# Modulation steps between the router's products, routing weights by f32r passes, and tokens in two f32r parts in the second expert stage

## The chip, the cores and the metric

The kernel runs on one core of a Trainium2 chip. The metric is the device time of one execution in microseconds (us), the median of several runs. A profile of one execution is at hand, with every instruction's start and duration.

## The reference, cut to what matters

A two-layer transformer over 256 latent and 256 context tokens, model width 1024, everything in float32. Layer 0 mixes tokens by window attention, layer 1 by differential attention, and each layer ends in a mixture of 32 experts of which every token uses two. All sub-layers are scaled and shifted by vectors that come out of a "modulation" product.

```
for i in range(2):
    mod  = (silu(c) @ mod_w[i] + mod_b[i]).reshape(6, D)        # shift, scale, gate, shift, scale, gate
    modc = (silu(c_ctx) @ mod_w[i] + mod_b[i]).reshape(6, D)
    h  = rmsnorm(x, g[i, 0]) * (1 + mod[1]) + mod[0]            # hc the same with modc
    y, yc = window_attention(...) if i == 0 else diff_attention(...)
    x = x + mod[2] * y
    h  = rmsnorm(x, g[i, 1]) * (1 + mod[4]) + mod[3]
    # hier_moe: best of 4 groups, two best of its 8 experts, softmax weights w1, w2
    x = x + mod[5] * sum over the token's two experts e of  w_e * (silu(u1) * u2) @ w_down[e],  [u1 u2] = h @ w_up[e]
return rmsnorm(x, final_g)
```

Layer 0 routes 512 tokens (latent and context), layer 1 only the 256 latent ones. Each expert's `w_up` is 1024 x 1024 and its `w_down` 512 x 1024, so one expert is 6.29 MB and one layer's experts are 201 MB.

## The kernel before, in words

**Memory.** SBUF holds an arena of 43 slots of 512 KB (128 partitions x 1024 floats). `Slot()` takes the slot that has been free longest, `free()` puts it at the end. Every weight block is one slot: `plan` is the list of all blocks in the order of use, and `stream.next()` issues the next block's load on SyncE's queue (line 177) into the slot it is given. A load waits until that slot's last reader is done, so how far loads run ahead of use is set by how many slots are free for them.

**Order.** Blocks of code under `tc.manual_schedule(engines=PE)` keep TensorE's instructions in the written order; elsewhere, and on the other engines everywhere, a planner orders them before the run.

**Modulation.** The first two sixths of layer 0 come first, in quarters. Then there are twelve steps in `mod_steps`, four for each third (m = 1, 2: the rest of layer 0; m = 3: shift and scale of layer 1's mixer). One step (`mod_step`, line 370) takes four slots of `mod_w` and makes 8 matmuls in four column strips of the array; a profile counts each float32 matmul as two records, so 16. After a third's last step, `mod_finish` copies the 128x512 sum out of PSUM, turns it by four transposes and adds the bias. Four steps run between the query projections (`QM`), eight inside the first layer's attention (`MODS = range(0, 24, 3)`, that is one in every third of its 24 units; three units are one head pair).

**Router and gather.** `Post` collects a layer's residual stream into 128-token tiles `tok[t]` while the output projection runs. Where a tile is kept in two slots, it is split into two float32r parts (high part by ScalarE, remainder by VectorE; layer 0's four tiles); where it is kept whole (`WHOLE[1] = (0, 1)`, both tiles of layer 1), it is one float32 copy. `moe` then computes logits, finds the experts by a chain of small VectorE operations, and makes ranks (line 1018) from which a 0/1 matrix P is built that picks up to 64 tokens for each of two experts. `gather` multiplies P with the tokens, half of the columns at a time (`half`, line 1152), scales or copies the result (1156 to 1162), turns it back (`spread_tokens`, 1198, 1200), and `gather_weights` (line 1188) multiplies P with the routing weights `WR` as float32 (two or three columns) and copies out one column for each expert (1191, 1193).

**Expert pair.** For each of 16 pairs in each layer: up products (`up`, 1209, 16 slots), `gate`, gather for the next pair, down products (`down`, 1252, 8 slots), weighting (1277, 1278), and `combine` (1291) back to all tokens with `gated_add` (509). At pair 5 a branch asks whether an expert has more than 64 tokens; here it isn't taken.

Of the kernel before, what the change touches and what calls it, by code (L numbers as in the profile page):

```python
# [12 lines left out]
F32 = mybir.dt.float32  # L13
# [12 lines left out]
KT = D // 128  # L26
# [15 lines left out]
WHOLE = ((), (0, 1))  # L42
FILL1 = ((1, 1, 1, 0), (0, 1, 1, 0))
QM = (1, 3, 5, 7)
MODS = range(0, 24, 3)
# [11 lines left out]
def _hybrid_dit(ctx, tc, a, out):  # L57
# [6 lines left out]
               for c, dt in (("f", F32), ("r", F32R))] for i in range(SLOTS)]  # L64
    const = ctx.enter_context(tc.tile_pool(name="const", bufs=1))
# [172 lines left out]
    for c in range(2):  # L238
        for k in range(4):
            plan_cols(wq0, 512 * c, (2 * k,))  # L240
            if 4 * c + k in QM:
                plan_mod(*todo.pop(0))
    while todo:
        plan_mod(*todo.pop(0))
    plan_out(a["win_w_o"][0])
# [58 lines left out]
    ident2 = const.tile([128, 64], F32, name="ident2")  # L304
# [3 lines left out]
    ident_b = const.tile([128, 128], BF, name="ident_b")  # L308
# [10 lines left out]
    for t, op in enumerate((OP.is_gt, OP.is_lt)):  # L319
        m = const.tile([128, 128], BF, name=f"mask_b{t}")  # L320
        ve.tensor_scalar(m, diff_f, 0.0, -BIG, op0=op, op1=OP.mult)
        mask_b.append(m)
# [56 lines left out]
    def mod_finish(l, third, halves, hb, acc):  # L379
        h0, nh = halves[0], len(halves)  # L380
        sb = row("q")
        ve.tensor_copy(sb[hb], acc[hb])
        tp = bank("G")
# [449 lines left out]
    tmp.free()  # L833
    rooms.pop().free()
# [21 lines left out]
    class Post:  # L856
        def __init__(self, l, nt, lb=None):
# [23 lines left out]
            homes[l].slot.free()  # L881
# [29 lines left out]
        def flip(self, h, tags, ks=range(4)):  # L911
            for t in range(self.nt):
# [7 lines left out]
                if t < 2 and len(self.tok[t]) > 1:  # L920
                    hi, lo = (v[:, hs] for v in self.tok[t])
                    se.activation(hi, ps[:, cs], AF.Copy)
                    ve.tensor_tensor(lo, ps[:, cs], hi.bitcast(F32), op=OP.subtract)
                elif self.nr == 1:
                    se.activation(self.slots[t][-1].f()[:, hs], ps[:, cs], AF.Copy, scale=self.ri[:, t:t + 1])
# [55 lines left out]

    def moe(l, nt, post, after, finish):
        T = nt * 128
        with tc.manual_schedule(engines=PE):
            lg = post.logits()
        post.shift(2, ge)
# [38 lines left out]
        WR = const.tile([128, nt, NE // 2, 3], F32, name=f"WR{l}", tag="WR")  # L1025
        W = WR[:, :, :, 0:2]
        cmi = const.tile([128, 1], I32, name=f"cmi{l}", tag="cmi")

        def weights():
# [22 lines left out]
            if not unit:  # L1052
                ve.tensor_copy(WR[:, :, :, 2], post.ri.unsqueeze(2).to_broadcast([128, nt, NE // 2]))
        h_slots, tok, unit = post.slots, post.tok, post.nr == 1

        np_ = NE // 2
        prev = st = None
        early_ks = range(0, KT // 2) if T == 512 else ()
        late_ks = range(len(early_ks), KT)
        for p in range(np_):  # L1060
# [17 lines left out]
            if p == IF_AT:  # L1078
# [6 lines left out]
                with tc.If(most > CAP):  # L1085
                    overflow(l, nt, key, W, None if unit else post.ri, tok, [hs_[k // 2].f(2, 512)[:, k % 2] for k in range(KT)])
# [39 lines left out]
    def gather(l, nt, p, key, WR, tok, unit, early=None, between=None, ri=None):  # L1126
# [10 lines left out]
        if ri is not None:  # L1137
            st["P"] = P
            if not unit:
                wps = bank("G")  # L1140
                for t in range(nt):
                    pe.matmul(wps[:, 0:1], P[:, t, :].bitcast(F32), ri[:, t:t + 1], start=(t == 0), stop=(t == nt - 1))
                ve.tensor_copy(st["w"][:, 1:2], wps[:, 0:1])
# [39 lines left out]

    def gather_weights(P, WR, p, st, n):
        wps = bank("G")
        nt = P.shape[1]
        for t in range(nt):
# [110 lines left out]
    def overflow(l, nt, key, W, ri, tok, hT):  # L1298
        T = nt * 128
        for t in range(nt):  # L1300
            for h in range(2):
# [13 lines left out]
                for k in range(4):  # L1315
# [3 lines left out]
        ve.scalar_tensor_tensor(Wov.rearrange("p t (a b) -> p t a b", b=2),  # L1319
                                key.rearrange("p t (a b) -> p t a b", b=2), float(CAP), W,  # L1320
# [484 lines left out]
```

## Time and profile before

| | |
|---|---|
| median of 3 runs | 1551.51 us (1550.75 to 1552.95) |
| the profiled execution's own time | 1550.44 us |
| its span, first to last instruction | 1548.8 us |
| mean granted TensorE clock | 0.981 of full speed |
| TensorE matmuls busy (PE) | 1458.1 us, 94% |
| VectorE (DVE), ScalarE (ACT), GpSimd (POOL) busy | 655.5, 384.6, 184.2 us |
| read from HBM | 483.16 MB, 313 GB/s over the span |

PE counts matmuls, PEld the loading of the stationary operand beside them. Busy times are unions; the ends of matmuls are modelled, so a row of matmuls is best read from the start of one group to the start of the next. "Idle before" names what an engine waited for.

### The profile page before, as it was taken

The page shows a single profiled execution, that of the slowest core. Times are in us where ns is not written, and L with a number is a line of the kernel's source. Part 1 is how long each engine was busy: PE and PEld are TensorE (multiplying, and loading weights), DVE is VectorE, ACT ScalarE, POOL GpSimd, SP SyncE. Part 2 cuts the span into 40 slices and gives each one's busy share as a digit, 9 for nine tenths or more (in the row PEclk, how much of TensorE's full clock was granted, in tenths as well). Part 3 has the DMA queues.
Part 4 walks back from the last instruction along what each step waited for, and adds up shares of the span by engine and source line. Part 5 has one row for each costly group of instructions (what it writes and reads, how often), then busy time and mean ns, then how long its engine had stood idle before and what let it go on. Part 6 is the DMA issues. An engine that isn't in the chain of part 4 may idle for free. (4 is left out here: it accounts for less than half of the span.)

```text
span 1548.8 us, 20271 instructions
## 1 busy us (share of the span) xinstructions
PE 1458.1 (94%) x7463; PEld 800.3 (52%) x7463; DVE 655.5 (42%) x1585; ACT 384.6 (25%) x823; POOL 184.2 (12%) x147
## 2 busy tenths in 40 slices
PE   6998999799999999999999899798999899999997
PEld 4765567445444454444545678684434333433444
DVE  3338862424333443333448726863323222322323
ACT  4426653211010011101115235652101010110112
POOL 2314551000000000000006463100000000000000
PEclk9999999899999999999998999999999999999999
DMA  9767225799989999999996532488999999999991
GB/s 330 243 214 273 82 86 187 278 366 401 395 343 393 401 398 398 391 397 403 382 297 229 182 124 71 161 284 304 387 409 409 409 408 409 409 409 409 409 394 68
DMA packets 169695, 485.67 MB, mean 314 GB/s; under 512 B 20825, under 2 KB 41586, under 8 KB 169586
## 3 DMA queue, kind: packets, MB, share of 16 engines
q1 hardware_dynamic: 169088, 483.66, 82.2%
q8 instruction: 63, 1.03, 0.3%
q10 hardware_dynamic: 498, 0.60, 0.1%
q14 instruction: 46, 0.38, 0.1%
HBM read 483.16 MB, written 1.05 MB: 313 GB/s over the span
## 5 line engine op out<-in xcount | busy, mean ns | idle before, releaser
L1209 PE MATMUL ps<-slotf,row 128*64 128x512 f32 x2048 | 449.2, 593 | 2.1 <-DVE row L1200 2.1
L1209 PEld LDWEIGHTS ps<-slotf,row 128*64 128x64 f32 x2048 | 145.2, 137 | 289.7 <-issue 274.4
L1252 PE MATMUL ps<-slotf,row 128*64 128x512 f32 x960 | 212.6, 595 | 0.0
L546 PE MATMUL ps<-slotr,slotr 128*128 128x512 f32 x768 | 193.4, 405 | 13.4 <-DVE slotf L1414 6.7
L509 DVE SCALAR_TENSOR_TENSOR slotf<-ps,mod,slotf 128x256 f32<-128x256 f32 x408 | 167.3, 477 | 62.3 <-PE ps L1291 29.7
L546 PEld LDWEIGHTS ps<-slotr,slotr 128*128 128x128 f32 x768 | 145.1, 194 | 50.4 <-DVE slotf L1414 7.1
L1252 PEld LDWEIGHTS ps<-slotf,row 128*64 128x64 f32 x960 | 66.3, 137 | 124.9 <-issue 118.9
L1216 ACT ACTIVATE row<-ps 128x512 f32<-128x512 f32 x30 | 17.9, 597 | 425.9 <-PE ps L1209 386.6
L1217 DVE SCALAR_TENSOR_TENSOR row<-row,ps 128x512 f32<-128x512 f32 x30 | 20.6, 687 | 234.4 <-ACT row L1216 234.3
L1278 DVE SCALAR_TENSOR_TENSOR row<-ps,ty,row 128x512 fp32r<-128x512 f32 x60 | 45.0, 750 | 176.5 <-ACT row L1277 173.3
L1277 ACT ACTIVATE row<-ps,ty 128x512 fp32r<-128x512 f32 x60 | 41.3, 688 | 263.0 <-PE ps L1252 262.7
L1291 PE MATMUL ps<-row,row 128*128 128x512 f32 (+1 forms) x512 | 104.4, 348 | 1.1 <-DVE slotf L509 1.0
L1291 PEld LDWEIGHTS ps<-row,row 128*128 128x128 f32 x512 | 77.3, 189 | 36.5 <-ACT row L1216 21.1
L521 POOL TENSOR_TENSOR slotr<-slotf,slotr 128x1024 fp32r<-128x1024 f32 x32 | 78.9, 2479 | 86.9 <-ACT slotr L517 72.1
L1200 DVE TENSOR_TENSOR row<-ps,mod 128x512 f32<-128x512 f32 x64 | 42.7, 686 | 101.7 <-PE ps L1198 100.9
L481 POOL TENSOR_TENSOR row<-row,row 128x512 f32<-128x512 f32 (+1 forms) x13 | 15.0, 1156 | 575.6 <-PE ps L1291 519.4
L1152 PE MATMUL ps<-slotf,row 128*128 128x512 f32 x128 | 65.0, 632 | 7.0 <-PEq L1085 4.7
L1152 PE MATMUL ps<-slotr,row 128*128 128x512 f32 x256 | 70.4, 419 | 0.0
L517 ACT ACTIVATE slotr<-slotf 128x1024 fp32r<-128x1024 f32 x44 | 45.9, 1055 | 63.1 <-DMA slotf<-in_diff_w_qkv 38.0
L1152 PEld LDWEIGHTS ps<-slotr,row 128*128 128x128 f32 x256 | 47.9, 198 | 10.0 <-issue 0.8
L1377 PE MATMUL ps<-slotr,slotr 128*128 128x512 f32 x192 | 47.6, 399 | 0.0
L1198 PE MATMUL ps<-ident,row 128*128 128x128 f32 x256 | 37.8, 280 | 7.5 <-DVE row L1156 6.7
(314 smaller groups left out, 1526.8 us busy)
## 6 DMA issues: line engine op xcount, KB each, us to landing
slotf<-in_moe_w_up SPq DMA_DIRECT2D x512, 512.0 KB, 9.5
slotf<-in_moe_w_down SPq DMA_DIRECT2D x256, 512.0 KB, 10.2
slotf<-in_mod_w SPq DMA_DIRECT2D x96, 512.0 KB, 6.3
slotf<-in_diff_w_qkv SPq DMA_DIRECT2D x24, 512.0 KB, 3.9
slotf<-in_win_w_qkv SPq DMA_DIRECT2D x12, 512.0 KB, 5.2
slotf<-in_win_w_o SPq DMA_DIRECT2D x8, 512.0 KB, 4.0
slotf<-in_diff_w_o SPq DMA_DIRECT2D x8, 512.0 KB, 4.1
slotf<-in_x SPq DMA_DIRECT2D x2, 512.0 KB, 4.1
```

The costliest lines, as they stand in the source:

```text
L509: ve.scalar_tensor_tensor(xT[k][:, sl], ps[:, sl], g[:, k, r:r + 1], xT[k][:, sl], op0=OP.mult, op1=OP.add)
L517: se.activation(hv, v, AF.Copy)
L521: (eng or (ge if split_i[0] % 3 == 0 else ve)).tensor_tensor(lv, v, hv.bitcast(F32), op=OP.subtract)
L546: pe.matmul(ps[t], h[:, x, ts], w[y][:, kk, :], start=(k + kk == 0 and n == 0), stop=(k + kk == KT - 1 and n == 2))
L1152: pe.matmul(g, P[:, t, :] if len(tok[t]) > 1 else P[:, t, :].bitcast(F32), v[:, hs], start=(t == 0 and i == 0), stop=(t == nt - 1 and i == ...
L1200: ve.tensor_tensor(o.rearrange("p (k c) -> p k c", k=4), ps.rearrange("p (k c) -> p k c", k=4), mods[l][:, 3, 4 * h:4 * h + 4, 0:1].to_bro ...
L1209: pe.matmul(u[h][64 * s:64 * s + 64, :], st["xt"][k // 4][:, c0:c0 + 64], w[s][1][:, h * 512:(h + 1) * 512], start=(k == 0), stop=(k == KT ...
L1252: pe.matmul(y[h][64 * s:64 * s + 64, :], acT[:, c0:c0 + 64], w[s][1][:, h * 512:(h + 1) * 512], start=(k == 0), stop=(k == 3))
L1277: se.activation(yh, y[h], AF.Copy, scale=wsl)
L1278: ve.scalar_tensor_tensor(yl, y[h], wsl, yh.bitcast(F32), op0=OP.mult, op1=OP.subtract)
L1291: pe.matmul(out, part[:, c * 128:(c + 1) * 128], st["PT"][:, :T], start=(i == 0), stop=(i == 1))
L1377: pe.matmul(ps, w[x][:, k % 4, ms], oT0[k][1][:, y, :], start=(k == 0 and i == 0), stop=(k == KT - 1 and i == 2))
```

## The change

- Four of the eight modulation steps leave the first layer's attention (`MODS` takes every sixth unit). Their 16 weight blocks are planned after the output projection's weights instead of before. In `moe` of layer 0 three of the four steps run right after the logits, in a bank of group A (`mods_meanwhile`), the fourth after the rank products (`last_mods`); its sum is copied by ScalarE, and `mod_turned` runs after the first gather. The slot `homes[0]`, which holds its bias, is freed after that instead of in `Post`.
- `WR` becomes float32r with a high and a low part; `gather_weights` is one float32r matmul for a tile, over 4 (layer 1) or 6 (layer 0) columns, in place of a float32 one. The two parts are added while they are copied out, by ScalarE with its accumulator (`add_parts`), in place of VectorE's copies. The factor 1/rms of layer 0's first pair goes the same way (`rr`).
- `WHOLE[1]` is empty: layer 1's two tiles are kept in two float32r parts in four slots instead of two, split from PSUM by ScalarE (with its scale) and VectorE (one `scalar_tensor_tensor`), and `half` takes two float32r matmuls for a tile instead of one float32 matmul.
- `ident2`, `ident_b` and the two masks move from storage of their own into one slot, `masks`, which is held from the start to the end of the first layer's attention.

```diff
-WHOLE = ((), (0, 1))
+WHOLE = ((), ())
-MODS = range(0, 24, 3)
+MODS = range(0, 24, 6)
...
+    while len(todo) > KT // 2:
+        plan_mod(*todo.pop(0))
+    plan_out(a["win_w_o"][0])
     while todo:
         plan_mod(*todo.pop(0))
-    plan_out(a["win_w_o"][0])
     plan_experts(0)
...
+    masks = Slot()
+    ident2 = masks.f()[:, 0:64]
...
     def mod_finish(l, third, halves, hb, acc):
-        h0, nh = halves[0], len(halves)
         sb = row("q")
         ve.tensor_copy(sb[hb], acc[hb])
+        mod_turned(l, third, halves, hb, sb)
...
-            homes[l].slot.free()
+            if not mod_steps:
+                homes[l].slot.free()
...
+                    if self.nr == 1:
+                        ri = self.ri[:, t:t + 1]
+                        se.activation(hi, ps[:, cs], AF.Copy, scale=ri)
+                        ve.scalar_tensor_tensor(lo, ps[:, cs], ri, hi.bitcast(F32), op0=OP.mult, op1=OP.subtract)
...
+    def mods_meanwhile():
+        while len(mod_steps) > 1:
+            mod_step("A")
+
+    def last_mods():
+        l, third, halves, hb, acc = mod_step("A").args
+
+        def moved():
+            sb = row("q")
+            se.activation(sb[hb], acc[hb], AF.Copy)
+            return partial(mod_turned, l, third, halves, hb, sb)
+
+        return moved
...
             lg = post.logits()
+            mods_meanwhile()
...
             pe.matmul(cps[:, 0:NE], ones_b, Mb[:, t, :], start=(t == 0), stop=(t == nt - 1))
-        WR = const.tile([128, nt, NE // 2, 3], F32, name=f"WR{l}", tag="WR")
-        W = WR[:, :, :, 0:2]
+        moved = last_mods() if mod_steps else None
+        cols = 2 if unit else 3
+        WR = const.tile([128, nt, NE // 2, 2, cols], F32R, name=f"WR{l}", tag="WR")
+        if not unit:
+            rr = const.tile([128, nt, 2], F32R, name=f"rr{l}")
+            ve.tensor_copy(rr[:, :, 0], post.ri)
+            ve.tensor_tensor(rr[:, :, 1], post.ri, rr[:, :, 0].bitcast(F32), op=OP.subtract)
...
+            hi, lo = WR[:, :, :, 0, :], WR[:, :, :, 1, :]
+            se.activation(hi, wide_w, AF.Copy)
+            ve.tensor_tensor(lo, wide_w, hi.bitcast(F32), op=OP.subtract)
...
+        turn_mods = moved() if moved else lambda: None
...
-                    st = gather(l, nt, 0, key, WR, tok, unit, weights, ri=post.ri)
+                    st = gather(l, nt, 0, key, WR, tok, unit, weights, ri=() if unit else rr)
+                    turn_mods()
+                    if moved:
+                        homes[l].slot.free()
...
+    def add_parts(dst, src):
+        n = src.shape[0]
+        se.activation(tiny("ap", [128, 2], bufs=2)[:n], src, AF.Copy, accum_out=dst)
+
     def gather_weights(P, WR, p, st, n):
...
-            pe.matmul(wps[:, 0:n], P[:, t, :].bitcast(F32), WR[:, t, p, 0:n], start=(t == 0), stop=(t == nt - 1))
+            pe.matmul(wps[:, 0:2 * c], P[:, t, :], WR[:, t, p], start=(t == 0), stop=(t == nt - 1))
+        v = wps[:, 0:2 * c].rearrange("p (b c) -> p c b", b=2)
         for s in range(2):
             pb = slice(64 * s, 64 * s + 64)
-            ve.tensor_copy(st["w"][pb, 0:1], wps[pb, s:s + 1])
+            add_parts(st["w"][pb, 0:1], v[pb, s])
         if n == 3:
-            ve.tensor_copy(st["w"][:, 1:2], wps[:, 2:3])
+            add_parts(st["w"][:, 1:2], v[:, 2])
```

## Rows read from the trace of the kernel before

**Rows 1.** The page: its first part (busy time, share of the span and instructions of each engine) and, of its second, the GB/s that the DMA engines moved in 40 equal slices of the span (38.7 us each).

```profile
PE 1458.1 (94%) x7463; PEld 800.3 (52%) x7463; DVE 655.5 (42%) x1585; ACT 384.6 (25%) x823; POOL 184.2 (12%) x147
...
GB/s 330 243 214 273 82 86 187 278 366 401 395 343 393 401 398 398 391 397 403 382 297 229 182 124 71 161 284 304 387 409 409 409 408 409 409 409 409 409 394 68
```

**Rows 2.** Busy time by stretch in the second layer's expert stage: the stretch in us from the span's start, its length, for each engine the busy us and (in brackets) instructions, then the granted TensorE clock as a share of full speed, the DMA engines' busy share, and GB/s.

```profile
1080.00:1120.00 40.00, 38.93 (x188) 17.17 (x188) 12.08 (x26) 4.70 (x9) 0.00 (x0) 1.00 0.98 389
1120.00:1480.00 360.00, 348.85 (x1676) 148.74 (x1674) 104.86 (x218) 41.41 (x74) 0.00 (x0) 1.00 1.03 409
...
1500.00:1512.00 12.00, 12.00 (x60) 4.57 (x62) 2.90 (x5) 1.37 (x2) 0.00 (x0) 1.00 1.02 350
1512.00:1516.00 4.00, 4.00 (x20) 1.29 (x18) 0.00 (x0) 0.00 (x0) 0.00 (x0) 1.00 0.67 221
```

**Rows 3.** The chain of waits that ended last, in the second expert stage: start us, length us, what (xcount). One pair of experts of sixteen, and the last pair's up products.

```profile
1259.13 2.10 PE ps L1291 x16
1261.23 1.73 PE ps L1152 x4
...
1263.05 0.61 ACT row L1158
...
1263.70 2.00 PE ps L1152 x4
...
1266.47 1.09 PE ps L1198 x8
...
1274.58 13.73 PE ps L1209 x64
1288.31 2.11 PE ps L1291 x16
...
1508.04 13.73 PE ps L1209 x64
```

**Rows 4.** Busy time by stretch in the first layer's attention; each stretch is one head pair with its three units. Columns as in rows 2; the last line holds sums and means over all four.

```profile
196.52:208.45 11.93, 11.93 (x87) 6.97 (x86) 10.03 (x27) 8.10 (x24) 6.97 (x6) 1.00 0.15 45
sum 47.71, PE 47.71 PEld 27.85 DVE 39.85 ACT 30.24 POOL 26.67; mean PE 11.93 PEld 6.96 DVE 9.96 ACT 7.56 POOL 6.67
```

**Rows 5.** Timeline of TensorE in the same stage, around one modulation step (line 370): start us, us, engine, line, operation, tiles, form, count.

```profile
203.82 1.04 PE L370 MATMUL ps<-slotf,slotf 128*32 128x512 f32 x2
204.79 0.66 PE L785 MATMUL ps<-ident,row 128*128 128x128 f32 x4
205.38 1.92 PE L370 MATMUL ps<-slotf,slotf 128*32 128x512 f32 x14
207.23 0.72 PE L748 MATMUL ps<-slotr,slotr 128*128 128x512 f32 x2
```

**Rows 6.** Timeline of the first layer's router and first gather. In brackets: idle us before it and what ended that.

```profile
281.73 1.19 PE L950 MATMUL ps<-ident,row 36*128 36x36 f32 x8 [0.46 <-ACT row L938]
...
291.02 0.18 PE L1018 MATMUL ps<-Mb,before_b 128*128 128x32 bf16 x1 [8.10 <-DVE Mb L1013]
...
292.65 1.84 PE L1142 MATMUL ps<-ri,row 128*128 128x1 f32 x8 [1.09 <-DVE s L1031]
...
294.35 3.76 PE L1152 MATMUL ps<-slotr,row 128*128 128x512 f32 x8
...
294.60 0.69 DVE L978 TENSOR_TENSOR slotr<-slotf,slotr 128x512 fp32r<-128x512 f32 x1
...
300.38 3.65 PE L1209 MATMUL ps<-slotf,row 128*64 128x512 f32 x16 [0.78 <-DVE row L1200]
```

**Rows 7.** Busy time by stretch across that router, columns as in rows 2.

```profile
284.40:298.05 13.65, 5.94 (x31) 4.98 (x31) 11.62 (x46) 4.05 (x8) 2.52 (x2) 0.50 0.70 272
```

**Rows 8.** Timeline of one gather of the first expert stage.

```profile
318.06 1.05 PE L1188 MATMUL ps<-WR,row 128*128 128x3 f32 x8
...
318.97 2.09 PE L1152 MATMUL ps<-slotr,row 128*128 128x512 f32 x8
...
320.90 0.60 PE L1168 MATMUL ps<-ident,row 128*128 128x128 f32 x4
321.15 0.69 ACT L1162 ACTIVATE row<-ps,ty 128x512 f32<-128x512 f32 x1 [3.21 <-PE ps L1152]
```

**Rows 9.** Busy time by stretch: one pair of the first expert stage, from its down products to the next pair's; columns as in rows 2.

```profile
356.10:387.90 31.80, 31.52 (x155) 15.12 (x154) 12.19 (x28) 3.86 (x6) 0.00 (x0) 1.00 1.01 399
```

**Rows 10.** Groups of instructions by line: busy us, mean ns of one | idle us before them.

```profile
L753 ACT ACTIVATION_READ_ACCUMULATOR row<-ps,ty 128x1 f32 x32 | 6.5, 203 | 0.0
...
L768 ACT ACTIVATE ty<-ty 128x2 f32<-128x2 f32 (+1 forms) x24 | 4.9, 204 | 0.0
```

**Rows 11.** Timeline of the second layer's router and first gather.

```profile
1051.54 2.42 ACT L925 ACTIVATE slotf<-ps,ri 128x512 f32<-128x512 f32 x4 [0.53 <-PE ps L917]
...
1054.76 0.23 DVE L1013 TENSOR_TENSOR Mb<-row,row 128x64 bf16<-128x64 f32 x1
...
1056.20 3.46 PE L1152 MATMUL ps<-slotf,row 128*128 128x512 f32 x4 [0.89 <-DVE s L1031]
...
1061.85 3.65 PE L1209 MATMUL ps<-slotf,row 128*64 128x512 f32 x16 [0.85 <-DVE row L1200]
```

**Rows 12.** Timeline of the loads that SyncE's queue issued (SP) in the first layer: start us, us over which the count was issued, line, tile<-input, count. These are loads of the first expert weights.

```profile
242.49 20.59 SPq L177 DMA_DIRECT2D slotf<-in_moe_w_up  x11
```

**Rows 13.** What the DMA queue (SP) waited for before it could issue the next load, from 0 to 120 us: total us, times, longest us.

```profile
SPq L177 <- PE ps L546: 35.8, 13, 5.7
```

More of the change, by code (lines that the diff above doesn't have):

```diff
@@ L64, in _hybrid_dit @@
                for c, dt in (("f", F32), ("r", F32R))] for i in range(SLOTS)]
+    halves = [nc.alloc_sbuf_tensor_at(f"slotb{i}", [128, 2048], BF, offset=base + 4096 * i).ap() for i in range(SLOTS)]
     const = ctx.enter_context(tc.tile_pool(name="const", bufs=1))
@@ L303, in _hybrid_dit @@
     make_identity(nc, ident)
-    ident2 = const.tile([128, 64], F32, name="ident2")
+    masks = Slot()
+    ident2 = masks.f()[:, 0:64]
+    masks_b = halves[masks.s].rearrange("p (a n) -> p a n", n=128)
     ve.tensor_tensor(ident2, ident[:, 0:64], ident[:, 64:128], op=OP.add)
@@ L307, in _hybrid_dit @@
     ve.memset(ones, 1.0)
-    ident_b = const.tile([128, 128], BF, name="ident_b")
+    ident_b = masks_b[:, 8]
     ve.tensor_copy(ident_b, ident)
@@ L319, in _hybrid_dit @@
     for t, op in enumerate((OP.is_gt, OP.is_lt)):
-        m = const.tile([128, 128], BF, name=f"mask_b{t}")
+        m = masks_b[:, 9 + t]
         ve.tensor_scalar(m, diff_f, 0.0, -BIG, op0=op, op1=OP.mult)
@@ L379, in mod_finish, with mod_turned @@
     def mod_finish(l, third, halves, hb, acc):
-        h0, nh = halves[0], len(halves)
         sb = row("q")
         ve.tensor_copy(sb[hb], acc[hb])
+        mod_turned(l, third, halves, hb, sb)
+    def mod_turned(l, third, halves, hb, sb):
+        h0, nh = halves[0], len(halves)
         tp = bank("G")
@@ L833, in _hybrid_dit @@
     tmp.free()
+    masks.free()
     rooms.pop().free()
@@ L1052, in weights @@
             if not unit:
-                ve.tensor_copy(WR[:, :, :, 2], post.ri.unsqueeze(2).to_broadcast([128, nt, NE // 2]))
-        h_slots, tok, unit = post.slots, post.tok, post.nr == 1
+                ve.tensor_copy(wide_w[:, :, :, 2], post.ri.unsqueeze(2).to_broadcast([128, nt, NE // 2]))
+            hi, lo = WR[:, :, :, 0, :], WR[:, :, :, 1, :]
+            se.activation(hi, wide_w, AF.Copy)
+            ve.tensor_tensor(lo, wide_w, hi.bitcast(F32), op=OP.subtract)
+        h_slots, tok = post.slots, post.tok
         np_ = NE // 2
         prev = st = None
+        turn_mods = moved() if moved else lambda: None
         early_ks = range(0, KT // 2) if T == 512 else ()
@@ L1085, in moe @@
                 with tc.If(most > CAP):
-                    overflow(l, nt, key, W, None if unit else post.ri, tok, [hs_[k // 2].f(2, 512)[:, k % 2] for k in range(KT)])
+                    overflow(l, nt, key, WR, None if unit else post.ri, tok, [hs_[k // 2].f(2, 512)[:, k % 2] for k in range(KT)])
                 for s in hs_:
@@ L1141, in gather @@
                 for t in range(nt):
-                    pe.matmul(wps[:, 0:1], P[:, t, :].bitcast(F32), ri[:, t:t + 1], start=(t == 0), stop=(t == nt - 1))
-                ve.tensor_copy(st["w"][:, 1:2], wps[:, 0:1])
+                    pe.matmul(wps[:, 0:2], P[:, t, :], ri[:, t, :], start=(t == 0), stop=(t == nt - 1))
+                add_parts(st["w"][:, 1:2], wps[:, 0:2])
         elif not unit:
```

16 lines of the change are left out of this document (10 added, 6 removed).

## The prediction, made before the changed kernel was run

> **What bounds the kernel now.** First the page: TensorE's matmuls are busy 94% of the span, so at first sight every matmul taken away is time won; but the GB/s slices rise to a flat 409 in the last quarter, and a flat line is a ceiling [rows 1]. So each stage has to be read by itself, and the last one first.
>
> *Second expert stage.* The stretches show 409 GB/s for 360 us on end at a DMA share of 1.03, with TensorE busy for 349 of them [rows 2]. Both look full. The chain settles which one is: it runs through TensorE and the short copies between its products, never through a load, and one pair takes 29.18 us (from 1259.13 to 1288.31) [rows 3]. A pair's 24 slots are 24 x 0.524 = 12.58 MB, at 409 GB/s 30.8 us. So TensorE uses weights faster than they arrive and lives on the slots loaded ahead. What is left of that lead at the end: after 1500 us the loads move 12 x 350 + 4 x 221 kB = 5.1 MB [rows 2]; the last eight slots (4.2 MB, down weights) are therefore still to come at about 1502.5, and the last up weights have landed then. Their matmuls start at 1508.04 + 7/8 x 13.73 = 1520.05 [rows 3]. The lead is 17.5 us: TensorE can win that much here and then waits for loads.
>
> *First layer's attention.* A head pair takes 11.93 us with TensorE busy throughout; VectorE needs 9.96 us of it, the others less [rows 4]. TensorE is the bound, VectorE next.
>
> *Router of layer 0.* TensorE idles 8.10 us while VectorE finds the experts, and then works at a granted clock of 0.50, that is 1.2 GHz: eight matmuls of line 1152 take 3.76 us [rows 6, 7], against 1.93 from start to next start at the full clock [rows 8].
>
> *First expert stage.* 31.8 us a pair, TensorE busy for 31.52 [rows 9]; loads would need 30.8, so TensorE bounds it, with 1 us to spare.
>
> **The change, part by part.** The sum is made against the profiled execution (1550.44 us, of which 1.64 lie outside the span), 1.07 below the median of the runs.
>
> *Four steps out of the attention.* One step costs TensorE 0.97 us (two records, 203.82 to 204.79) and 1.85 (fourteen, 205.38 to 207.23): 2.82 [rows 5], so 11.3 for four. But a head pair without a step has 9.11 us of matmuls and VectorE 9.96 on average [rows 4]. If VectorE then sets the pace, each saves 1.97. I take that, -7.9; ends -11.3 and -4 (half of it, since scores, softmax and transposes of a unit follow one another and the steps also filled such waits).
>
> *The steps in the router.* Three run in the 8.10 us of idling (3 x 1.85 = 5.6), hidden by VectorE's chain; without that cover they would cost their 5.6. The fourth, 1.85, comes after the rank products, ends near 293.4 and holds up the product behind it (line 1142, start 292.65 before) by 0.7. For the gain: with TensorE at work in the gap I expect the full clock afterwards. Line 1142 then takes under 0.5 instead of 1.84; the gather's remainder for the last tile is ready at 294.60 + 0.69 = 295.3, so its eight products end near 295.8 instead of 298.1 [rows 6]. VectorE's two extra small operations (`rr`) take back 0.3. Term -1.9. If the clock falls all the same, the fourth step (3.7 us at 1.2 GHz) pushes all behind it: +1.6. The turning (four transposes) falls into the wait for VectorE that ends at 300.38 [rows 6]. The 16 mod loads take the places of the first 16 expert loads in SyncE's queue; eleven of those places were issued from 242.49 to 263.08 [rows 12], 20 us ahead of the router, so the steps find their weights. The expert loads behind them come 16 x 1.28 = 20.5 us of transfer later, but the four steps free their slots before the first pair starts, and the first stage's loads need 30.8 us a pair of 31.3: no starving, cost 0.
>
> *Routing weights.* In the first stage line 1188 takes 0.91 us for eight records (318.06 to 318.97) [rows 8]. Four float32r matmuls of 6 columns: no such row; from below 0.114 a record as here, from above 0.131 as line 1291's 256 columns (2.10 us for 16, [rows 3]). I take 0.46, gain 0.45 a pair, 15 pairs: -6.8 (bounds -5.8 and, at half a record's time, -10). The copies move from VectorE (off the path) to ScalarE, each an ACTIVATE and an accumulator read, 0.204 + 0.203 us [rows 10]; three are 1.2 us. Who waits: the scaling (1162) for the third, and the transposes of P (1168) for the bank. Both also wait for the first half's eight products, 1.93 us [rows 8], so 1.2 is hidden; without this cover it would be up to 0.7 a pair.
>
> *Two parts in the second stage.* Each half of a gather is four float32 records, 1.73 us [rows 3]; four float32r matmuls go by 1.93/8 = 0.24 each [rows 8], 0.97. In a pair the way from the first half's start to the turning back (1261.23 to 1266.47, 5.24 us [rows 3]) becomes 0.97, then the six transposes that the copy of 0.61 hid (0.9), 0.97, and copy and issue 0.76: 3.6. TensorE alone saves 1.65 x 15 pairs and 0.9 in the first: 25.6. Loads don't allow it. The lead is 17.5; two slots fewer for loads (four for tokens) put the last load 2 x 1.28 = 2.6 us later; and the loads, no longer held up by slots in the first pairs (389 for 409 GB/s over 40 us [rows 2]), win 2.0 back. Term -17.0 (ends -14 and -19.5).
>
> *Router of layer 1.* No steps here. The first half-gather, 3.46 us at the low clock [rows 11], is halved: -1.7. The remainders are new on VectorE: four of 128x512, 0.69 each by line 978's row [rows 6], ready as ScalarE's four copies end between 1052.1 and 1054.0, in the midst of the chain that ends with Mb at 1054.76 [rows 11]. If the planner puts them in as they become ready, +2.8. I take both: +1.0 (ends -1.7 and +2.8).
>
> *The slot for masks* leaves one less until the attention ends: 0, since TensorE isn't held up by loads there; rival below. The rest costs nothing: the wider copies of `WR` are made while the first up products run.
>
> Sum: -7.9 - 1.9 - 6.8 - 17.0 + 1.0 = -32.6. 1550.44 - 32.6 = 1517.8, on the runs' median 1518.9; I say **1519**.
>
> **Rivals.**
>
> *A: loads give way.* If they ran faster once slots come free sooner, the second stage would give all of TensorE's 25.6 instead of 17.0: 1510. Against it, 409 flat at share 1.03 over 360 us [rows 2]. The Trainium skill (HBM Reference, Specifications) gives about 425 GB/s for a core streaming alone, and 358 as its share. By 425 a layer's 201 MB would come 18 us sooner (an estimate from that page) and this rival would hold; the trace's 409 lies between the two and decides.
>
> *B: the attention gives nothing.* VectorE or the units' own waits take the steps' place, above all near the start where a step covers a wait: 1519 + 7.9 = 1527. For it, VectorE's 9.96 of 11.93 [rows 4]; against it, its share would be 100%.
>
> *C: the steps lengthen the router.* If their loads could start only as the logits are turned (281.73 [rows 6]), 20.5 us of transfer end at 302, the last step starts 10 us later than at 291.5, and the steps are on the path: +10, 1529. Against it, [rows 12].
>
> *D: slower.* The masks' slot is missing in the query projections, where SyncE waited 13 times for slots that line 546 frees, 35.8 us in all, 5.7 at most [rows 13]. If each of eight weight blocks then came 5.7 us later with TensorE waiting, +45.6: 1565. It decides from 32.6/8 = 4.1 us a block, if none of it is cover. Against it, no wait of TensorE for a load there.
>
> **How the numbers follow.** Chances: forecast 0.64, A 0.06, B 0.15, C 0.08, D 0.04, gains that cancel to no change 0.03. Within 0.2% (3.1 us, about what a measurement here can tell from none): 0.03. Slower: D and 0.01 of C's tail, 0.05. Faster: 0.92. The forecast's own ends, put together as independent, are 1513 to 1525; with B and C at 1527 and 1529, and A at 1510, the range is 1509 to 1531.
>
> **What would show it.** Right: head pairs without a step near 10 us; granted clock 1.00 in most of the first router; four records of line 1188's successor in about 0.46 us; pairs of the second stage near 27.6 us until the last one or two, where TensorE waits for `in_moe_w_up`, with 409 GB/s from the stage's start. Wrong: any wait of TensorE for loads before the last third of that stage; pairs that stay at 29 us; pairs of the first stage at 32; a wait for `in_mod_w` in the router; projections held up before 115 us.

## The result

The changed kernel takes 1526.12 us (median; 1522.09 to 1528.14), the kernel before beside it 1551.76: a ratio of 0.9831, 95% interval 0.9809 to 0.9853. On a second chip it was 0.9837 (0.9824 to 0.985). The forecast was 1519 with a range of 1509 to 1531. So the sign and the range held, and of the 32.6 us that the terms add up to, some 26 came.

The page of the changed kernel: its first part and the GB/s of the second, as in [rows 1] (40 slices, here of 38.2 us).

```profile
PE 1431.4 (94%) x7363; PEld 793.2 (52%) x7363; DVE 649.0 (43%) x1512; ACT 410.4 (27%) x986; POOL 184.8 (12%) x147
...
GB/s 326 222 223 139 42 56 193 346 409 409 409 409 408 408 409 409 409 409 408 402 315 228 173 124 83 133 278 265 394 409 409 408 409 409 409 409 409 409 409 199
```

TensorE has 26.7 us less of matmuls, ScalarE 25.8 us more. The flat 409 GB/s now fills both expert stages.

By stages, each taken from the start of a first product to the start of the next stage's (us; the second execution is of the same kernel, `e5_same_again` below):

| stage | before | changed | second execution | change | forecast |
|---|---|---|---|---|---|
| start to the first scores of the attention | 115.53 | 116.20 | 113.08 | +0.7 / -2.5 | 0 |
| attention and out-projection, to the logits' turning | 166.20 | 165.30 | 163.77 | -0.9 / -2.4 | -7.9 |
| router of layer 0 | 18.65 | 17.19 | 17.17 | -1.5 | -1.9 |
| first expert stage, to the start of its last pair | 481.0 | 470.6 | 470.7 | -10.4 | -6.8 |
| from there to layer 1's first up product | 280.5 | 281.5 | 281.5 | +1.1 | +1.0 |
| second expert stage, to the last pair's down products | 463.7 | 452.4 | 452.6 | -11.3 | -17.0 |
| the end | 23.2 | 23.2 | 23.2 | 0 | 0 |

The profiled execution of the changed kernel is the slowest of its runs; in its out-projection the clock was at 0.50 for 3.41 us, which the second execution doesn't show, and that is most of what sets the two apart there.

**Attention.** Busy time by stretch, one head pair each, columns as in [rows 4]; then TensorE's timeline around one modulation step, as in [rows 5] (lines have moved: the step is 375 now, scores 756, transposes 793 and 800, value products 815).

```profile
149.44:160.24 10.80, 10.34 (x72) 6.59 (x71) 9.24 (x29) 7.25 (x23) 6.12 (x6) 1.00 0.00 1
160.24:172.18 11.94, 11.94 (x83) 6.94 (x82) 8.44 (x24) 7.27 (x23) 6.12 (x6) 1.00 0.07 20
...
195.49:207.71 12.22, 9.89 (x69) 6.50 (x68) 12.22 (x37) 8.34 (x24) 6.13 (x6) 1.00 0.11 39
```

```profile
155.77 1.04 PE L375 MATMUL ps<-slotf,slotf 128*32 128x512 f32 x2
156.75 0.66 PE L793 MATMUL ps<-ident,row 128*128 128x128 f32 x4
...
159.65 0.66 PE L800 MATMUL ps<-ident,slotf 128*128 128x128 f32 x4 [0.34 <-POOL slotf L797]
...
166.57 1.05 PE L375 MATMUL ps<-slotf,slotf 128*32 128x512 f32 x4
...
168.14 1.90 PE L375 MATMUL ps<-slotf,slotf 128*32 128x512 f32 x10
```

Before, each pair of [rows 4] held a whole step and took 11.93. Now pairs with 14 of a step's 16 records (the second line) alternate with pairs that hold only the next step's first two (the first line). A step is cut in three places, 2 + 4 + 10 records, 0.98 + 0.98 + 1.83 from start to start: 3.8 us where it took 2.82. Its eight matmuls go to four column strips that work side by side, and one matmul alone (the first two records) takes as long as two together (the next four). The last pair holds no step and still takes 12.22, with VectorE busy throughout.

**Router of layer 0.** Timeline of TensorE, as in [rows 6], and the stretch, as in [rows 7].

```profile
281.50 1.19 PE L963 MATMUL ps<-ident,row 36*128 36x36 f32 x8 [0.46 <-ACT row L951]
282.62 6.20 PE L375 MATMUL ps<-slotf,slotf 128*32 128x512 f32 x50
290.31 0.18 PE L1047 MATMUL ps<-Mb,before_b 128*128 128x32 bf16 x1 [1.50 <-DVE Mb L1042]
...
290.74 1.92 PE L375 MATMUL ps<-slotf,slotf 128*32 128x512 f32 x14
292.59 0.61 PE L1185 MATMUL ps<-rr,row 128*128 128x2 f32 x4
293.06 1.86 PE L1195 MATMUL ps<-slotr,row 128*128 128x512 f32 x7
295.61 0.50 PE L1195 MATMUL ps<-slotr,row 128*128 128x512 f32 x1 [0.69 <-DVE slotf L987]
...
298.69 1.51 PE L1258 MATMUL ps<-slotf,row 128*64 128x512 f32 x6 [0.60 <-DVE row L1249]
```

```profile
282.00:298.69 16.69, 13.51 (x108) 6.26 (x107) 14.10 (x60) 5.77 (x14) 2.55 (x2) 1.00 1.03 411
```

The three steps lie in VectorE's chain, the clock stays at 1.00, no step waits for a load.

**First expert stage.** One gather in the second pair: TensorE's timeline and VectorE's in the kernel before, and TensorE's in the changed one.

```profile
349.64 0.95 PE L1188 MATMUL ps<-WR,row 128*128 128x3 f32 x8
350.45 2.09 PE L1152 MATMUL ps<-slotr,row 128*128 128x512 f32 x8
352.84 0.63 PE L1168 MATMUL ps<-ident,row 128*128 128x128 f32 x4 [0.30 <-DVE ty L1193]
353.30 0.60 PE L1240 MATMUL ps<-ident,row 128*128 128x128 f32 x4
```

```profile
349.46 2.83 DVE L509 SCALAR_TENSOR_TENSOR slotf<-ps,mod,slotf 128x256 f32<-128x256 f32 x7
352.21 0.31 DVE L1191 COPY ty<-ps 64x1 f32<-64x1 f32 x2
352.54 0.16 DVE L1193 COPY ty<-ps 128x1 f32<-128x1 f32 x1
```

```profile
347.60 0.51 PE L1236 MATMUL ps<-WR,row 128*128 128x6 f32 x4
347.96 2.11 PE L1195 MATMUL ps<-slotr,row 128*128 128x512 f32 x8
349.91 0.60 PE L1211 MATMUL ps<-ident,row 128*128 128x128 f32 x4
```

The weights take 0.36 from start to next start, 0.81 before. And a wait has gone that the forecast didn't have: VectorE's three copies stood behind seven additions, and the transposes of P waited 0.30 for the last of them.

**Second expert stage.** The chain of waits of the changed kernel, as in [rows 3]: one pair, and the last two.

```profile
1398.53 13.73 PE ps L1258 x64
...
1426.22 13.73 PE ps L1258 x64
...
1453.92 12.88 PE ps L1258 x58
...
1466.82 10.18 DMA slotf<-in_moe_w_down
...
1477.06 10.17 DMA slotf<-in_moe_w_up
...
1487.29 10.24 DMA slotf<-in_moe_w_up
...
1497.57 1.93 PE ps L1258 x6
```

A pair takes 27.69 us (1398.53 to 1426.22) in place of 29.18. From 1466.8 on the chain no longer runs through TensorE: it runs from load to load, each 10.2 us from issue to landing, until the last up weights are there at 1497.5. Pair 5, with the branch, was slower than before, 39.44 us against 35.59, at a clock of 0.50 for 13.65 us:

```profile
1212.58:1226.23 13.65, 9.24 (x30) 6.35 (x32) 3.78 (x6) 2.69 (x8) 0.00 (x0) 0.50 1.03 408
```

### The profile page after: what moved, and what is told of

Its sections match the earlier page's. It is cut to its first block, busy times and chain, and to the rows that moved or that the text cites. A ratio compares the mean times of both kernels' runs of the same rounds, so it can differ in the third digit from the quotient of the medians.

```text
span 1526.5 us, 20170 instructions
## 1 busy us (share of the span) xinstructions
PE 1431.4 (94%) x7363; PEld 793.2 (52%) x7363; DVE 649.0 (43%) x1512; ACT 410.4 (27%) x986; POOL 184.8 (12%) x147
## 5 line engine op out<-in xcount | busy, mean ns | idle before, releaser
L1258 PE MATMUL ps<-slotf,row 128*64 128x512 f32 x2048 | 455.0, 596 | 3.3 <-DVE row L1249 2.6
L1301 PE MATMUL ps<-slotf,row 128*64 128x512 f32 x960 | 213.5, 597 | 0.0
L1195 PE MATMUL ps<-slotr,row 128*128 128x512 f32 x384 | 109.1, 420 | 7.5 <-PEq L1125 4.7
L1195 PEld LDWEIGHTS ps<-slotr,row 128*128 128x128 f32 x384 | 69.9, 195 | 28.8 <-PEq L1125 4.9
L489 POOL TENSOR_TENSOR row<-row,row 128x512 f32<-128x512 f32 (+1 forms) x13 | 15.5, 1196 | 562.3 <-PE ps L1340 508.1
L1247 PEld LDWEIGHTS ps<-ident,row 128*128 128x128 f32 x256 | 29.3, 145 | 29.6 <-issue 13.8
## 6 DMA issues: line engine op xcount, KB each, us to landing
slotf<-in_moe_w_up SPq DMA_DIRECT2D x512, 512.0 KB, 10.2
slotf<-in_moe_w_down SPq DMA_DIRECT2D x256, 512.0 KB, 10.2
```

Source lines behind the costliest of these rows:

```text
L1195: pe.matmul(g, P[:, t, :] if len(tok[t]) > 1 else P[:, t, :].bitcast(F32), v[:, hs], start=(t == 0 and i == 0), stop=(t == nt - 1 and i == ...
L1247: pe.transpose(ps[:, k * 128:(k + 1) * 128], st["x"][h][:, k * 128:(k + 1) * 128], ident)
L1258: pe.matmul(u[h][64 * s:64 * s + 64, :], st["xt"][k // 4][:, c0:c0 + 64], w[s][1][:, h * 512:(h + 1) * 512], start=(k == 0), stop=(k == KT ...
L1301: pe.matmul(y[h][64 * s:64 * s + 64, :], acT[:, c0:c0 + 64], w[s][1][:, h * 512:(h + 1) * 512], start=(k == 0), stop=(k == 3))
```

## The experiments

Two questions were open. In most of the expectations theory 1 holds the forecast's terms; theory 2 says that the attention can't use the room that the steps leave, and that loads end the second stage earlier in the lead than forecast. Edits are to the changed kernel where nothing else is said; line numbers move a little from kernel to kernel.

### Each part undone

```diff
-MODS = range(0, 24, 6)
+MODS = range(0, 24, 3)
...
-    while len(todo) > KT // 2:
-        plan_mod(*todo.pop(0))
-    plan_out(a["win_w_o"][0])
     while todo:
         plan_mod(*todo.pop(0))
+    plan_out(a["win_w_o"][0])
```

> The changed kernel with the four moved modulation steps put back into the attention, at the places and in the load order that they had before; the other parts of the change stay. Theory 1 (the prediction's terms): the head pairs with a step take 11.93 us again in place of 9.96 and the first router falls back to the clock of 0.50, so 9.8 us more than the changed kernel, near 1536 us. Theory 2 (what the two traces side by side suggest): the attention of the changed kernel won only about 2 us, of which a dip of the clock in the output projection took most, and the router 1.5: 2 to 3.5 us more, 1528 to 1530 us; out-projection starts some 2 us later than in the changed kernel's trace, and the first up products some 3.5 us later.

Measured: 1528.95 us, 0.9868 (0.9852 to 0.9883) of the kernel before, so 5 to 6 us above the changed kernel's 0.983, between the two theories. From the first scores to the router 167.7 us, against 163.8 and 165.3: 2.4 to 3.9 more. The router again ran at a clock of 0.50:

```profile
284.50:298.20 13.70, 6.40 (x32) 5.05 (x32) 11.67 (x47) 5.25 (x12) 2.52 (x2) 0.50 0.74 286
```

But it took 17.70 us, not 18.65. So TensorE's idling there goes with the low clock, as [rows 7] had it, and the steps lift it. With the float32r passes for 1/rms the router already gains 0.95 of its 1.5 us at the low clock; `e3_f32_weights` below shows the other order.

```diff
-WHOLE = ((), ())
+WHOLE = ((), (0, 1))
...
+                elif self.nr == 1:
+                    se.activation(self.slots[t][-1].f()[:, hs], ps[:, cs], AF.Copy, scale=self.ri[:, t:t + 1])
```

> The changed kernel with layer 1's two tiles of tokens kept whole in two slots and multiplied as float32, as before; the other parts stay. Theory 1 (the prediction's terms -17.0 and +1.0): 16 us more, near 1542 us. Theory 2 (the side-by-side reading: the stage won 11.3, the router of layer 1 lost 1.1): 10 us more, near 1536 us, with pairs of 29.2 us, the pair with the branch near 35.6, and no wait of TensorE for loads at the end of the stage.

Measured: 1542.95 us, 0.9955 (0.9941 to 0.9969), 18 to 19 us more than the changed kernel by the ratios. That is nearer theory 1's 16 than theory 2's 10, and above what this part alone gives (`e6_two_parts_alone` below). The profiled execution (1538.25, the fastest of its runs, 4.7 under their median) shows less of it: the second stage takes 467.9 us, 15.3 to 15.5 more, and what lies between the stages 2.0 less. The stage is 4.2 longer here than in the kernel before, though both hold the tokens whole: the first pair 32.80 against 31.05 (the clock was at 0.50 until 3.2 us into it, in the kernel before it had risen ahead of the stage), the pair with the branch 37.15 against 35.59, thirteen others 0.07 each. So the other parts cost this stage 2 to 3 us beside the clock's, which loads cover in the changed kernel and nothing covers here.

```diff
-        WR = const.tile([128, nt, NE // 2, 2, cols], F32R, name=f"WR{l}", tag="WR")
+        WR = const.tile([128, nt, NE // 2, 3], F32, name=f"WR{l}", tag="WR")
...
-            pe.matmul(wps[:, 0:2 * c], P[:, t, :], WR[:, t, p], start=(t == 0), stop=(t == nt - 1))
+            pe.matmul(wps[:, 0:n], P[:, t, :].bitcast(F32), WR[:, t, p, 0:n], start=(t == 0), stop=(t == nt - 1))
...
-            add_parts(st["w"][pb, 0:1], v[pb, s])
+            ve.tensor_copy(st["w"][pb, 0:1], wps[pb, s:s + 1])
```

> The changed kernel with the routing weights as one float32 matmul a tile and VectorE's copies, as before; the other parts stay. Theory 1 (the prediction's term): pairs of the first expert stage 0.45 us longer, 6.8 in all, near 1533 us. Theory 2 (the side-by-side reading, pairs 31.77 against 31.10 and the pair with the branch 37.23 against 35.76): 0.67 a pair and 10 in all, near 1536 us. In the second stage nothing by either, if loads set that stage's end.

Measured: 1534.24 us, 0.9907 (0.9892 to 0.9922), 11 to 12 us more; pairs of 31.77, the first stage 481.2 us. Theory 2's size. The second stage takes 451.6, as in the changed kernel, though its branch pair is 5.0 shorter (34.42).

The edit also takes back the float32r form of 1/rms in the router, and the router takes 17.17 us all the same. Two lines of its timeline there:

```profile
288.61 1.05 PE L1176 MATMUL ps<-ri,row 128*128 128x1 f32 x8
289.52 2.44 PE L1186 MATMUL ps<-slotr,row 128*128 128x512 f32 x8
```

The product for 1/rms takes 0.91 us to the next start, 0.47 in the changed kernel, but the products behind it don't wait, where TensorE waits 0.69 us for VectorE's remainder (line 987) in the changed kernel. So the steps, with the full clock behind them (1.00 from 282.2 us on), give the router's 1.5 us alone, and beside them the float32r form adds nothing.

### What ends the second stage

```diff
-                most = nc.values_load(cmi[0:1, 0:1], min_val=0, max_val=T)
-                with tc.If(most > CAP):
-                    overflow(...)
+                if l == 0:
+                    most = nc.values_load(cmi[0:1, 0:1], min_val=0, max_val=T)
+                    with tc.If(most > CAP):
+                        overflow(...)
```

> The changed kernel without the branch at pair 5 of the second expert stage: the read of the counter and the branch around the code for more than 64 tokens are left out there (the slots reserved for it still are); the first stage keeps its branch. Theory 1 (loads set the end of the stage): the pair loses its extra 5 us of stall and low clock, but TensorE waits for loads that much longer in the last pairs; the loads end 448 us after the stage's first up products as they do now, and the time stays within 1 us of the changed kernel's. Theory 2 (the branch's stall is part of what is missing from the forecast): 5 us less, near 1521 us, with pair 5 at 34 us.

Measured: 1525.0 us, 0.9839 (0.9826 to 0.9853): no change. Pair 5 took 30.32 us, 9 less, and the stage 450.4 instead of 452.4; from the twelfth pair on the pairs took 29.2 to 30.7, that is the pace of the loads. Theory 1 of this experiment, almost to the full: the branch and its low clock are paid by waits that would come anyway.

Even the 2.0 us need not be the branch's: `e9_half_steps` below has it (pair 5 at 39.32 us), and its stage takes 450.0. What those two share is a first pair of 28.9 us, 31.2 in the changed kernel. The first 20 us of the stage, changed kernel and this one, columns as in [rows 2]:

```profile
1050.81:1070.81 20.00, 19.27 (x78) 6.96 (x79) 3.22 (x10) 1.48 (x6) 0.00 (x0) 0.88 0.75 279
```

```profile
1047.91:1067.91 20.00, 19.17 (x90) 8.11 (x90) 3.17 (x7) 2.69 (x8) 0.00 (x0) 1.00 0.86 318
```

In the changed kernel, and in its second execution, the clock is at 0.50 as the stage starts; TensorE does less, slots come free later, and fewer bytes arrive.

```diff
+        hold = [Slot(), Slot()] if unit else []
...
-            for s in itertools.chain(*h_slots):
+            for s in itertools.chain(hold, *h_slots):
```

> The changed kernel with two slots of the arena taken and left unused from the start of layer 1's router to the last pair of the second expert stage; no work is added. Theory 1 (loads set the end of that stage and every slot is 1.28 us of lead): the stage takes 2.6 us longer, 454 us, all of it waits for loads in the last three pairs. Theory 2 (TensorE, the branch and the clock set it): no difference, 451.5 us.

Measured: 1528.31 us, 0.9856 (0.9841 to 0.9871). The stage took 455.1 us against 452.6 on the same chip: theory 1's 2.6, but for 0.1. The last load of the stage was issued 452.5 us after the first up product, 450.0 in the changed kernel. A slot is 1.28 us here, and nothing else was touched. The chain runs through loads for the last 41 us:

```profile
1455.80 10.18 DMA slotf<-in_moe_w_up
...
1486.52 10.23 DMA slotf<-in_moe_w_up
...
1496.80 1.93 PE ps L1259 x6
```

The kernel before with nothing but the tokens in two parts:

```diff
-WHOLE = ((), (0, 1))
+WHOLE = ((), ())
...
+                    if self.nr == 1:
+                        se.activation(hi, ps[:, cs], AF.Copy, scale=ri)
+                        ve.scalar_tensor_tensor(lo, ps[:, cs], ri, hi.bitcast(F32), op0=OP.mult, op1=OP.subtract)
```

> The kernel before with one part of the change alone: layer 1's two tiles in two float32r parts in four slots; the steps, the routing weights and the masks stay as before. Theory 1 (the prediction's terms -17.0 and +1.0): 16 us less than before. Theory 2 (loads set the stage's end, and the lead of loads was overrated): the stage from the first up product to the last pair's end takes 451 us in place of 463.6, the router of layer 1 1 us more, in all 11 to 12 us less than before.

Measured: 1538.56 us, 0.9922 (0.9909 to 0.9936), 12 us less than before. Stage 452.4, router of layer 1 and what lies ahead of it 1.2 longer. Theory 2. Its pairs took 27.60 and its branch pair 33.62, the lead was gone by the thirteenth pair, and the stage ended as in the changed kernel: 452.4 both times.

The changed kernel itself, beside the last two and the next one:

> The changed kernel as it is, on the chip on which the other three of this group run: the measure for them. Both theories: a ratio to the kernel before of 0.981 to 0.985, as it had.

Measured: 1526.03 us, 0.9837 (0.9824 to 0.985).

### What a head pair of the attention needs

```diff
-QM = (1, 3, 5, 7)
-MODS = range(0, 24, 6)
+QM = range(8)
+MODS = ()
```

> The changed kernel with the last four modulation steps of the attention moved as well, into the query projections (a step after every block of them in place of every second one); none is left in the attention. Theory 1 (a remaining step costs 3.8 us because the planner cuts its eight matmuls into three places, and a head pair without any of it takes 9.9 us, as forecast from VectorE): six head pairs near 9.9 to 10.2 us, the attention 13 us shorter than in the changed kernel, the projections 7.7 us longer (4 x 1.92), 5 us less in all. Theory 2 (the chain through VectorE and GpSimd needs 10.8 us and more for a head pair, whether there is a step or not): head pairs of 10.8 to 12.2 us, the attention 8 us shorter, nothing in all.

Measured: 1529.06 us, 0.9854 (0.9839 to 0.9869), 2.6 us more than the changed kernel. Head pairs without any step take 10.75 us, so theory 2, though not by its sum: the attention, from its first scores to its last value products, got 4.4 us shorter and not 8. Two of the pairs took longer, 11.34 and 11.50, the second with VectorE busy for 11.35 of it. Busy time by stretch, and what TensorE waited for in the first of these pairs (total us, times, longest):

```profile
165.93:176.67 10.74, 9.47 (x70) 6.53 (x69) 8.69 (x26) 7.15 (x23) 6.11 (x6) 1.00 0.01 2
...
188.17:198.91 10.74, 9.48 (x69) 6.53 (x69) 8.69 (x26) 7.15 (x23) 6.11 (x6) 1.00 0.15 50
```

```profile
PE ps L800 <- POOL slotf L797: 1.3, 2, 0.9
```

No engine is full: VectorE 8.69 of 10.74, TensorE 9.47, GpSimd 6.11. What TensorE waits for is the last unit's scaling on GpSimd, the end of a row of dependent operations (scores, maximum, exponential, reciprocal, scaling). So, with the 9.11 us of matmuls that the prediction worked out for a pair, a pair hides 10.75 - 9.11 = 1.64 us of other products for nothing, and a whole step is 2.82.

```diff
-                ge.tensor_tensor(ev, ev, ri[:, j, :].unsqueeze(2)
+                (ve if j else ge).tensor_tensor(ev, ev, ri[:, j, :].unsqueeze(2)
```

> The changed kernel with one of the two scalings of each head pair's third unit moved from GpSimd to VectorE (eight instructions of 128x512 in all). Theory 1 (GpSimd's two scalings in a row are what TensorE waits for at the end of a pair without a step): pairs without a step 0.4 to 0.9 us shorter than 10.8, pairs with a whole step 11.95 as before, since TensorE is busy throughout; 1 to 2 us less in all. Theory 2 (the prediction's: VectorE sets the pace of a pair without a step): VectorE gets two to three quarters of a us more in each pair, and those pairs get longer by that, 11.4 us.

Measured: 1524.22 us, 0.9831 (0.9818 to 0.9845), as the changed kernel. Pairs without a whole step took 10.83 and 11.46, in place of 10.80 and 10.93:

```profile
145.13:155.96 10.83, 10.83 (x71) 6.95 (x70) 10.73 (x27) 7.18 (x23) 5.67 (x5) 1.00 0.00 1
...
167.68:179.14 11.46, 10.89 (x71) 6.89 (x70) 11.27 (x28) 7.40 (x23) 5.63 (x5) 1.00 0.25 81
```

My expectation that this wait alone sets the 10.75 fell. With the scaling on VectorE, that engine is full (10.73 of 10.83), and two limits lie close together. TensorE's row shows it busy throughout as well (with the next step's first two records in the pair), so which of the two sets the 10.83 isn't shown.

Half a step in every pair instead of a whole one in every second:

```diff
-MODS = range(0, 24, 6)
+MODS = range(0, 24, 3)
...
+        def products(kk):
+            for j, w in ws:
+                pe.matmul(acc[32 * j:32 * j + 32, :], cs[:, k + kk, :], w[1][:, kk, :],
+                          start=(k + kk == 0), stop=(k + kk == KT - 1))
...
-        mod_run(i in MODS)
+        if i in MODS:
+            mod_half()
```

> The changed kernel with its four remaining steps in the attention cut into halves of four matmuls each, one half in every head pair (units 0, 3, ..., 21) in place of a whole step in every second one. Theory 1 (a head pair can't be shorter than 10.75 us, because TensorE waits for GpSimd's scaling of the last unit, so that it hides 1.64 us of other products for nothing; a whole step is 2.82 and costs the difference): a half takes 0.97 + 0.95 = 1.92 us in the planner's order, so every pair takes 9.11 + 1.92 = 11.0 us, in place of 10.8 and 11.95 by turns: 2 us less than the changed kernel. Theory 2 (the last head pair's stretch, where VectorE finishes the modulation and splits a weight block, sets it): pairs shorter, but the two last ones longer by as much, nothing in all.

Measured: 1522.57 us, 0.981 (0.9794 to 0.9826), by the ratios 3 to 4 us less than the changed kernel (the intervals touch), 29 less than the kernel before; whether it is faster than the changed kernel these times don't settle. Every pair is full, near the 11.0 of theory 1:

```profile
158.22:169.31 11.09, 11.09 (x77) 6.72 (x77) 8.98 (x27) 7.28 (x23) 6.12 (x6) 1.00 0.01 1
...
191.50:202.95 11.45, 11.45 (x81) 7.08 (x80) 9.60 (x27) 8.12 (x24) 6.23 (x7) 1.00 0.12 35
```

From the first value products to the last 82.2 us, 83.8 in the changed kernel; the last full pair 11.45 in place of 12.22, since VectorE's work behind the last step falls into the stretch after it, which is 1.2 longer (14.8 against 13.6). In all that is 1.6 us of the attention, near theory 1's 2; the second stage is 2.6 shorter through its start, as said above, and the first 1.4 longer.

Both edits at once:

> The last two kernels' edits together. Theory 1 (TensorE's own 9.11 us and the 1.92 of a half step are all that a pair has to hold, once GpSimd's wait is shorter): pairs of 11.0 us, 2 us less than the changed kernel. Theory 2 (VectorE): its 9.24 and 0.7 more a pair leave pairs above 11.4 us, no gain.

Measured: 1528.05 us, 0.9855 (0.984 to 0.987), 5.5 us slower than half steps alone and 3.8 slower than the scaling alone, by the medians. Pairs of 11.82 and 12.20, and TensorE is full in them:

```profile
145.20:157.02 11.82, 11.82 (x77) 6.88 (x76) 11.55 (x31) 7.41 (x24) 5.12 (x5) 1.00 0.01 2
157.02:169.22 12.20, 12.20 (x77) 6.99 (x76) 11.24 (x29) 7.28 (x23) 5.63 (x5) 1.00 0.01 1
```

These are theory 2's numbers, but VectorE alone doesn't explain them: TensorE's records are as many as in the half-step kernel (77), and take 0.7 to 1.1 us more. In the planner's order for this kernel the value products of a head pair are cut as the steps are: by turns the first of eight stands apart from the other seven, or the first of four from the other three. That this makes up the whole difference wasn't tried, and the attention isn't all of it: this profile has the clock at 0.50 for 6.83 us in the router, which takes 18.85 us, 17.18 in the half-step kernel.

## Why the prediction was right, and where it was wrong

**What ends the second expert stage: right.** After the change its chain passes through loads at its end, at 409 GB/s, and five kernels with quite different branch pairs (30.3 to 39.5 us) end that stage within 450.0 to 452.6 us. Rival A, faster loads, is out: the slices show 408 and 409 GB/s once the stage is under way. The 425 GB/s that the Trainium skill gives (HBM Reference, Specifications) was not reached.

**Two parts in the second stage: mechanism right, -17.0 measured -11.3.** TensorE's saving was nearly as worked out, 1.49 a pair for 1.65. The mis-sized term is the lead. The forecast let the last 5.1 MB arrive slot after slot and so had the last up weights landed at 1502.5. But a load takes 10.2 us from issue to landing while others run beside it:

```profile
1485.39 10.57 SPq L177 DMA_DIRECT2D slotf<-in_moe_w_up  x9
```

```profile
slotf<-in_moe_w_up SPq DMA_DIRECT2D x12, 512.0 KB, 10.2
```

These are two views of the kernel before: SyncE's timeline with its last loads of up weights, and the loads from 1480 to 1515 us with their median time from issue to landing. The nine were issued 1.28 apart, the last at 1495.63, so it landed near 1505.8; the lead was 1520.05 - 1505.8 = 14.2, not 17.5. The two slots cost their 2.6 (`e8` measures 2.5 for two more). The 2.0 that the loads were to win back did not come here: the loads don't run at 409 from the stage's start (279 GB/s in the first 20 us, at the low clock shown at `e4_no_branch`), and the last load is issued 450 us after the first up product, 447 before. 14.2 - 2.6 = 11.6, measured 11.3. Where the first pair had the full clock (`e1`, `e4`, `e9`, `e10`, `e11`), the stage took 450.0 to 451.5, so up to 2.4 us were to be had. Why `e6`, with that clock too, took 452.4 stays open.

**Attention: wrong, -7.9 measured -2.7** from the first scores to the last value products (107.75 to 105.08 us), and -4.3 against `e1_steps_back` (109.43), which differs in the steps and their loads' order alone. The step that failed is "If VectorE then sets the pace": busy time was taken for the time that a pair needs. VectorE is busy 8.69 us in a pair without steps, and the pair takes 10.75. Of the four removed steps two gave 1.0 to 1.1 us, the one ahead of the first value products 0.6 (with 3.41 us at a clock of 0.50 there, which the kernel before doesn't have; 1.2 to 1.3 against `e1_steps_back`, which has it too), and the last next to nothing: the turning behind a third's last step (0.44 of TensorE) moved into a pair that was already full, and the VectorE work that follows it, with a split of the out-projection's weights, fell into the last pair, which no longer had a step to cover it and took 12.22. Rival B, at 1527, came nearer to the time than the forecast, but its mark, VectorE at 100%, holds only for that last pair.

**Router of layer 0: -1.9 measured -1.5, in the way forecast.** The steps hide, the clock stays at 1.00, no load is late (rival C is out). The product behind the fourth step went from 1.70 us (292.65 to 294.35 in [rows 6]) to 0.47, and the gather then waits for VectorE's remainder, as the forecast had it. So two gains don't add up here: the full clock with the steps gives the 1.5 without the float32r form (`e3_f32_weights`), the float32r form 0.95 without the clock (`e1_steps_back`).

**Routing weights: -6.8 measured -10.4.** The product's 0.45 a pair is exact (0.81 to 0.36). "The copies move from VectorE (off the path)" is what failed. They were on it: from the starts of the lines' groups in a later pair, the gather's products with the wait behind them fall from 4.31 to 3.91 us, of which 0.20 comes back between the next transposes (0.36 to 0.56). Net 0.66 a pair. [rows 8] is the first pair's gather, where no addition of the pair before stands in VectorE's queue; in all later pairs but the one at the branch seven do. The pair with the branch adds 0.8 beside the 0.66, most likely through its clock: low for 6.8 us before, 3.4 in the changed kernel, and 37.11 us again with 6.8 in `e1_steps_back`.

**Router of layer 1: +1.0 measured +1.1,** and both of its parts came: the four remainders stand in VectorE's chain ahead of `Mb`, and the first half-gather takes 2.04 us in place of 3.46 [rows 11].

```profile
1041.64 2.72 DVE L935 SCALAR_TENSOR_TENSOR slotr<-ps,ri,slotr 128x512 fp32r<-128x512 f32 x4
```

```profile
1046.11 2.04 PE L1195 MATMUL ps<-slotr,row 128*128 128x512 f32 x4 [0.89 <-DVE s L1067]
```

**The masks' slot: 0;** the attention's start moved by what two executions of one kernel differ by, so rival D is out.

The errors offset in part: 5.2 us short in the attention and 5.7 in the second stage, 3.6 over in the first. The time lies past the forecast's own ends (1513 to 1525); the range held it because rivals B and C had widened it, and the first stage's surplus brought it nearer by luck.

## What to carry to other kernels

The busy time of the next engine is not the time that a loop takes whose steps depend on each other; before a filler is removed, ask what time the loop takes when it is only itself, and spread what is left of the filler evenly, since each turn hides a fixed amount and no more. Read the cost of a moved small operation from a steady-state turn of the loop, not from the first. A lead of loads over use ends where the last load lands, which is its time in flight after its issue; and once loads ended the stage here, a further 9 us off TensorE's work in it gained 2 us at most (`e4`), while two buffer slots were worth two loads (`e8`).

## What the runs showed of the hardware that was not expected

- One matmul in one of four column strips takes as long as two or more side by side: 0.98 us for one of the modulation's matmuls and for two, 1.83 for five, 1.85 for seven [rows 5]. The Trainium skill (TensorEngine Tiling (Array Packing), Key Properties) says that a change of the tiling mode drains the engine, and each cut adds two such changes; how much of the 0.98 that is, no run here shows.
- A 512 KB load took 10.2 us from issue to landing where the queue moved 409 GB/s, that is 1.28 us a load.
- The code behind the second stage's branch isn't run, and the pair still takes 6 to 12 us more than a plain one, with the clock at 0.50 for 3.41 to 13.65 us about it. With the branch left out (`e4_no_branch`) 2.6 of these 11.75 us remain, and the trace shows no low stretch there. The stretch is 13.65 us in the changed kernel, 6.83 without its float32r weights (`e3`), 3.41 with whole tokens (`e2`) and in the kernel before; why stays open.
